# A two-layer hybrid transformer kernel: two attention blocks under way, more gate products beside the convolution, modulation over the remaining gate products

## The chip, the cores and the metric

The kernel runs on one core of a Trainium2 chip. The metric is the device time of one execution in microseconds (us), taken as the median of several runs. A core has a matrix engine (PE, with its weight loads shown as PEld), a vector engine (DVE), a scalar engine (ACT), a general engine (POOL) and a queue that issues DMA transfers (SP). Each works through its own list of instructions in order; they meet at semaphores.

## What is computed

Two layers over 512 latent tokens and 256 context tokens of width 1024, in float32. Each layer first mixes tokens with three branches that share one input projection, then runs an MLP. Layer 1, the last, computes the latent tokens alone in its mixing and MLP. Cut to the mixing sub-layer:

```python
h = layer_norm(x) * (1 + scale) + shift            # scale, shift: sections of silu(c) @ w_mod
u_pool, u_q, u_k, u_v, u_conv, u_gate = split(h @ w_in + b_in)
y_pool = pool_mixer(u_pool) @ w_pool_out
o      = attention(u_q, u_k, u_v)                  # 8 heads of 64 on 2 key/value heads
y_attn = o @ w_attn_out                            # latents: blocks of 128 queries, keys of the
                                                   # neighbouring blocks and all 256 context keys
y_conv = swish(layer_norm(depthwise_conv31(a * sigmoid(b)))) @ w_conv_out
g_pool, g_attn, g_conv = split(sigmoid(u_gate))
y = (g_pool * y_pool + g_attn * y_attn + g_conv * y_conv) @ w_out
x = layer_norm(alpha * x + gate * y) * g + b
```

The gates are 3 x 1024 columns of the input projection. The modulation has six sections (0 to 5) per layer; sections 3 and 4 are the shift and scale ahead of the MLP, and section 2 is the gate of the mixing sub-layer.

## The kernel before, in words

Every float32 matrix product is made of three products of rounded parts (high x high, high x low, low x high). A unit of weights is 128 x 512 floats: SP loads it into one of five `raw` buffers (L133), ACT rounds the high part `wh` (L138), and POOL or DVE subtracts to get the low part `wl` (L141). `wh` and `wl` live in a ring of `NRING` = 9 buffers each; in the MLP phase 4 (layer 0) or 6 (layer 1) more are added.

The order on PE is written out by hand: PE does the program's order. The other engines' orders are made by a planner at compile time. PE's program order comes from a counter of matmul columns, `pe["t"]` (L523 to L551): `tick` advances it, `later(cols, steps)` puts a piece of work into a heap that is due so many columns later, and `pace(steps, every)` issues one step of a list each time `every` columns have gone by.

In a mixing phase (`w_phase`, L559), `other` (L641) is a list of filler for PE: first the 8 gate tiles of the attention branch, then for every tile of 128 output channels the pool gate with the pool product and the convolution gate with the convolution product. One gate tile is 8 x 3 matmuls of 512 columns, and in layer 0 of 256 more. `cover(cols)` runs filler for so many columns.

The stages of a mixing phase, in PE's order:

- projections of values, keys, queries and pool;
- the depthwise convolution on DVE (L318 to L329, 31 taps). PE runs filler meanwhile: `cover(W_CONV0)` in layer 0 and `cover(W_CONV1)` in layer 1 (L739). Then come `pool_products` (L718), which for two tiles load a 128 x 128 weight (L721), split it on DVE and POOL and multiply (L730 to L732), and `conv_norm` (L331);
- attention: per key/value head four latent blocks (`attn_lat`) and, in layer 0, two context blocks (`attn_ctx`): 12 blocks in layer 0 and 8 in layer 1. A block's scores go through four heads: matmuls into one of two PSUM tiles `S` of 1024 columns, a maximum (L510) and `negm` (L511) on DVE, an exponential on ACT (L514). `softmax_pv` (L415) scales the four rows `P` (L424, L426), transposes them on PE into the same two `S` tiles (L435), splits them on ACT and DVE (L448, L449), and multiplies by the values into one bank `po` of the pool `psa` (L451, L452). One block is under way at a time: a block yields a number of columns, and `cover` fills them (L764). Ahead of the second head group the queries are projected (L761 to L763);
- `drain(other)` (L766) runs what filler is left;
- the final step (`fin`, L772 to L788): for each of 8 tiles, the attention product with the stored gate (`sgd`) and the stored sum of the other two branches (`mfd`) is added into A. In layer 0 the matmuls of modulation sections 3 and 4 (L189, 16 loads `wm` of 512 KB, 18 steps) are paced through these products, one step every 7000 columns, and the rest follows at once (L785).

PSUM has eight banks: two in `psa` (branch products, `po`, small things), two in `psg` (gate products), four as the two `S` tiles.

Of the kernel before, what the change touches and what calls it, by code (L numbers as in the profile page):

```python
# [10 lines left out]
F32 = mybir.dt.float32  # L11
F32R = mybir.dt.float32r
AF = mybir.ActivationFunctionType
ALU = mybir.AluOpType
# [24 lines left out]
NRING = 9  # L39

W_S0 = 0
W_S1 = 5200
W_S2 = 1800
W_S3 = 10000
W_PT = 4000
W_CN = 10000
W_PV = 1400
# [13 lines left out]
W_Q = 0  # L61
W_F = 2000
# [10 lines left out]
W_CONV0 = 134000  # L73
W_CONV1 = 90000
# [7 lines left out]
def backbone(ctx: ExitStack, tc: tile.TileContext, I: dict, out: bass.AP):  # L82
# [332 lines left out]
    def softmax_pv(pp, pss, g, Pt, vtiles, negm, sums, V_, sink, dst, qsl):  # L415

        es = pp.tile([P, 4], F32, tag="es", name=uid("es"), bufs=2)
        V.tensor_add(es, negm, sink[:, 4 * g:4 * g + 4])
        S.activation(es, es, AF.Exp)
        V.tensor_add(es, es, sums)  # L420
        V.reciprocal(es, es)
        for a in range(4):
            if a == 3:
                S.mul(Pt[a], Pt[a], es[:, a:a + 1])  # L424
            else:
                V.tensor_scalar(out=Pt[a], in0=Pt[a], scalar1=es[:, a:a + 1], scalar2=None, op0=ALU.mult)  # L426
        yield W_S3
        pts = []

        def transposes(ns):  # L430
            big = pss.tile([P, 1024], F32, tag="S", name=uid("pt"))
            for n in ns:
                pt = big[:, (n % 2) * 512:(n % 2 + 1) * 512]
                for a in range(4):
                    T.transpose(pt[:, a * P:(a + 1) * P], Pt[a][:, n * P:(n + 1) * P], ident)  # L435
                pts.append(pt)

        nt = len(vtiles)
        for n in range(0, min(nt, 4), 2):
            transposes(range(n, min(n + 2, nt)))  # L440
        yield W_PT
        po = bank()
        for n, vt in enumerate(vtiles):
            if n == 2 and nt > 4:
                transposes((4,))
            ph = pp.tile([P, 512], F32R, tag="pth", name=uid("pth"), bufs=2)
            pl = pp.tile([P, 512], F32R, tag="ptl", name=uid("ptl"), bufs=2)
# [12 lines left out]
        sl = (slice(None), slice(4 + 2 * g, 6 + 2 * g), qsl)  # L460
        split(dst[0][sl], dst[1][sl], ot[:, :, :], V, G)

    def attn_ctx(pp, pss, g, nb, Q, KH, KL, V_, nsink, sink, dst):

        qsl = slice(TL + nb * P, TL + (nb + 1) * P)
        s = pss.tile([P, 1024], F32, tag="S", name=uid("S"))
        for a in range(4):
            o = s[:, a * 256:(a + 1) * 256]
            T.matmul(o, Q[a][:, qsl], KH[g][:, CS], start=True, stop=False)
            T.matmul(o, Q[a][:, qsl], KL[g][:, CS], start=False, stop=True)  # L470
        negm = pp.tile([P, 4], F32, tag="ngm", name=uid("ngm"), bufs=2)
        mx = pp.tile([P, 4], F32, tag="mx", name=uid("mx"), bufs=2)
# [3 lines left out]
        sums = pp.tile([P, 4], F32, tag="sums", name=uid("sums"), bufs=2)  # L476
        Pt = []
        for a in range(4):
            p = pp.tile([P, 640], F32, tag="P", name=uid("P"), bufs=4)
            S.activation(p[:, :256], s[:, a * 256:(a + 1) * 256], AF.Exp, bias=negm[:, a:a + 1],  # L480
                         scale=SCALE, accum_out=sums[:, a:a + 1])
            Pt.append(p[:, :256])
        yield from softmax_pv(pp, pss, g, Pt, [4, 5], negm, sums, V_, sink, dst, qsl)

    def attn_lat(pp, pss, g, n, Q, KH, KL, V_, nsink, sink, dst, masks):
# [6 lines left out]
        negm = pp.tile([P, 4], F32, tag="ngm", name=uid("ngm"), bufs=2)  # L492
        mx = pp.tile([P, 4], F32, tag="mx", name=uid("mx"), bufs=2)
        sums = pp.tile([P, 4], F32, tag="sums", name=uid("sums"), bufs=2)
        Pt = []
        for a in range(4):
# [16 lines left out]
            p = pp.tile([P, 640], F32, tag="P", name=uid("P"), bufs=4)  # L513
# [3 lines left out]
            if a < 3:  # L517
                yield (W_S0, W_S1, W_S2)[a] + (W_F if a == 1 and n == 0 else 0)
# [40 lines left out]
    def w_phase(i, A, B, has_ctx, pre, todo):  # L559
# [5 lines left out]
        with ExitStack() as ph:  # L565
# [8 lines left out]
            mg = ph.enter_context(tc.tile_pool(name=f"mg{i}", bufs=4, reuse_waits="tile"))  # L574
# [27 lines left out]
            def gate_steps(m, b, w2=None, ks=()):  # L602

# [4 lines left out]
                for _, sl in outs_all:  # L608
# [3 lines left out]
                    if w2:  # L612
                        yield from branch_steps(w2, ks, ks[0], g, [(0, sl)], psa)
                return g

            def branch_steps(w, ks, w0, g, outs, pool):

                assert ks[0] in mixed
# [6 lines left out]
            def gated_steps():  # L625
# [14 lines left out]
            mixed = set()  # L640
# [111 lines left out]
            def blocks(g):  # L752
                for n in range(4):
                    yield from attn_lat(pp, pss, g, n, Q, KH, KL, V_, nsink, sink, B, masks)
                    if has_ctx and n % 2:
                        yield from attn_ctx(pp, pss, g, n // 2, Q, KH, KL, V_, nsink, sink, B)

            for g in range(NKV):
                if g:
                    Q = [kv.tile([P, W], F32R, tag=f"q{a}", name=uid("q")) for a in range(4)]  # L760
                    for jj in range(2):  # L761
                        query(Q, g, jj, pp.tile([P, TL], F32, tag="rt", name=uid("rt"), bufs=1))
                        cover(W_Q)  # L763
# [4 lines left out]
            mix.close()  # L768
            pace(None, 0)
# [408 lines left out]
```

## Time and profile before

| | us |
|---|---|
| median of 3 runs (1996.89, 1997.4, 2002.95) | 1997.4 |
| the profiled execution's own time | 1999.35 |
| its span, first to last instruction | 1997.6 |
| PE busy | 1852.4 (93%) |
| DVE busy | 1204.1 (60%) |
| POOL busy | 771.6 (39%) |
| ACT busy | 733.1 (37%) |

PE is the engine to read: a stretch in which it is idle, or runs at a granted clock below 1, is time that the span holds and no product needs. Matmuls are pipelined, so that one of 512 columns shows some 390 ns while the next starts 227 ns after it.

### The profile page before, as it was taken

The numbers are of one execution on the slowest core, as the hardware profiler recorded it, in microseconds if no ns is written. First come the engines' busy times: TensorE is split into PE (matmuls) and PEld (weight loads), VectorE is DVE, ScalarE is ACT, GpSimd is POOL, SyncE is SP. The second block draws the span as 40 slices with busy tenths as digits, with TensorE's granted clock in tenths as the row PEclk, the third lists the DMA queues.
The fourth block names the chain that finished last, engine by engine and source line by source line (L and its number), as shares of the span: only waits on it lengthen the run. The fifth ranks groups of instructions, "written<-read, shape, count | busy, mean of one in ns | idle before, by whom it ended". The sixth has DMA issues, their size and how long they took to land. (4 is left out here: it accounts for less than half of the span.)

```text
span 1997.6 us, 27087 instructions
## 1 busy us (share of the span) xinstructions
PE 1852.4 (93%) x9910; PEld 1554.4 (78%) x9910; DVE 1204.1 (60%) x2066; ACT 733.1 (37%) x1359; POOL 771.6 (39%) x630
## 2 busy tenths in 40 slices
PE   5999899998899999999999988978998989999997
PEld 4788788787678888888788868856876768888886
DVE  6489555564468946765533584886566694333356
ACT  4422245344234432232133254324545354332331
POOL 3752432332435322222222557644342554332343
PEclk9999899999999999999999989989999999999999
DMA  8523111113775434554422422231223653332331
GB/s 305 185 89 111 61 59 46 56 59 113 278 233 173 168 110 122 171 192 161 155 66 86 137 86 87 75 123 63 70 64 101 232 200 116 100 96 90 98 124 43
DMA packets 117558, 244.94 MB, mean 123 GB/s; under 512 B 14608, under 2 KB 16944, under 8 KB 117424
## 3 DMA queue, kind: packets, MB, share of 16 engines
q1 hardware_dynamic: 117424, 243.21, 37.4%
q8 instruction: 77, 1.26, 0.3%
q14 instruction: 57, 0.47, 0.1%
HBM read 223.20 MB, written 19.96 MB: 122 GB/s over the span
## 5 line engine op out<-in xcount | busy, mean ns | idle before, releaser
L141 POOL TENSOR_TENSOR wl<-raw,wh 128x512 fp32r<-128x512 f32 x372 | 517.1, 1401 | 830.9 <-ACT wh L138 803.9
L138 ACT CAST wh<-raw 128x512 fp32r<-128x512 f32 x506 | 310.4, 621 | 620.9 <-PE ps L171 282.0
L160 PE MATMUL ps<-actbh,wh 128*128 128x512 f32 (+1 forms) x1016 | 352.5, 347 | 2.8 <-ACT qf L661 1.9
L160 PE MATMUL ps<-actbl,wh 128*128 128x512 f32 (+1 forms) x1016 | 349.1, 344 | 4.0 <-POOL actbl L255 4.0
L160 PE MATMUL ps<-actbh,wl 128*128 128x512 f32 (+1 forms) x1016 | 348.1, 343 | 0.0
L160 PE MATMUL ps<-actah,wh 128*128 128x512 f32 (+1 forms) x928 | 331.7, 357 | 13.4 <-ACT actah L252 5.7
L160 PE MATMUL ps<-actal,wh 128*128 128x512 f32 (+1 forms) x928 | 327.6, 353 | 2.6 <-POOL actal L255 1.4
L160 PE MATMUL ps<-actah,wl 128*128 128x512 f32 (+1 forms) x928 | 327.1, 352 | 0.0
L160 PEld LDWEIGHTS ps<-actbh,wh 128*128 128x128 f32 x1016 | 196.1, 193 | 31.1 <-issue 4.9
L160 PEld LDWEIGHTS ps<-actbl,wh 128*128 128x128 f32 x1016 | 195.8, 193 | 25.6 <-POOL actbl L255 4.8
L160 PEld LDWEIGHTS ps<-actbh,wl 128*128 128x128 f32 x1016 | 195.2, 192 | 22.4
L160 PEld LDWEIGHTS ps<-actah,wh 128*128 128x128 f32 x928 | 177.7, 191 | 42.3 <-ACT actah L252 6.1
L160 PEld LDWEIGHTS ps<-actal,wh 128*128 128x128 f32 x928 | 177.5, 191 | 25.4 <-POOL actal L255 2.0
L160 PEld LDWEIGHTS ps<-actah,wl 128*128 128x128 f32 x928 | 177.4, 191 | 23.6
L169 PE MATMUL ps<-wh,actah 128*128 128x512 f32 x480 | 192.1, 400 | 3.4 <-DVE acc L926 2.0
L170 PE MATMUL ps<-wl,actah 128*128 128x512 f32 x480 | 189.6, 395 | 0.0
L171 PE MATMUL ps<-wh,actal 128*128 128x512 f32 x480 | 189.0, 394 | 0.5 <-DVE actal L255 0.5
L141 DVE TENSOR_TENSOR wl<-raw,wh 128x512 fp32r<-128x512 f32 x134 | 126.8, 947 | 88.8 <-ACT wh L138 88.4
L208 DVE SCALAR_TENSOR_TENSOR wm<-wm,sc,wm 128x512 f32<-128x512 f32 x140 | 120.9, 895 | 65.7 <-DMA wm<-in_wmod 65.7
L919 DVE TENSOR_TENSOR acc<-ps,acc 128x512 f32<-128x512 f32 x140 | 94.9, 684 | 93.6 <-PE ps L171 93.6
L169 PE MATMUL ps<-wh,actbh 128*128 128x512 f32 (+1 forms) x328 | 127.1, 387 | 2.2 <-DVE fg L622 2.2
L171 PE MATMUL ps<-wh,actbl 128*128 128x512 f32 (+1 forms) x328 | 126.8, 386 | 0.0
(207 smaller groups left out, 2735.2 us busy)
## 6 DMA issues: line engine op xcount, KB each, us to landing
raw<-in_w SPq DMA_DIRECT2D x264, 256.0 KB, 3.2
raw<-in_win SPq DMA_DIRECT2D x154, 256.0 KB, 2.9
wm<-in_wmod SPq DMA_DIRECT2D x72, 512.0 KB, 4.2
raw<-in_wout SPq DMA_DIRECT2D x56, 256.0 KB, 3.0
wm<-in_wmod SPq DMA_DIRECT2D x48, 256.0 KB, 5.2
raw<-in_wbr SPq DMA_DIRECT2D x32, 256.0 KB, 2.7
x1d<-R SPq DMA_DIRECT2D x10, 512.0 KB, 2.6
acc<-in_b SPq DMA_DIRECT2D x10, 512.0 KB
```

The lines of the kernel that those rows point to most:

```text
L138: S.copy(wh, r)
L141: e.tensor_tensor(out=wl, in0=r, in1=wh[:].bitcast(F32), op=ALU.subtract)
L160: T.matmul(ps, w(hl, w0 + n), x[xi][:, k, sl], start=(start and first and hl == 0 and xi == 0), stop=(stop and last and hl == 1))
L169: T.matmul(ps, x[0][:, k0 + k, tsl], wh, start=(k == 0), stop=False)
L170: T.matmul(ps, x[0][:, k0 + k, tsl], wl, start=False, stop=False)
L171: T.matmul(ps, x[1][:, k0 + k, tsl], wh, start=False, stop=(k == n - 1))
L208: V.scalar_tensor_tensor(out=o, in0=x, scalar=sc[:, k, r:r + 1], in1=o, op0=ALU.mult, op1=ALU.add)
L919: V.tensor_add(a, ps, a)
```

## The change

- The two layers' cover beside the convolution becomes 145000 (from 134000) and 118000 (from 90000) columns.
- Attention no longer runs one block after the other under `cover`. `launch` starts a block as soon as fewer than two are under way and no other is in its scores; a block's steps go into the heap (`later`) with their waits; only one block at a time is in its products (transposes and value products), another that comes to them is held. PE takes filler step by step while anything is due. The transposes and value products go in pairs of key tiles. `P` has 8 buffers instead of 4, `negm`, `mx` and `sums` 3 instead of 2.
- A gate tile is now done as a whole, and its branch product follows over both streams; before, each stream's branch product came right behind that stream's gate product.
- In layer 1 the pool gates run two tiles ahead, and the buffers of the gates grow from 4 to 6.
- The weight ring has 7 buffers instead of 9.
- The filler left after attention is no longer drained before `fin` is opened: sections 3 and 4 are paced (every 9000 columns) over that filler and the final products.

```diff
-NRING = 9
+NRING = 7
-W_S0 = 0
-W_S1 = 5200
-W_S2 = 1800
-W_S3 = 10000
-W_PT = 4000
+W_S = 3500
+W_S3 = 12000
+W_PT = 5000
-W_PV = 1400
+W_PV = 1800
-W_CONV0 = 134000
-W_CONV1 = 90000
+W_CONV0 = 145000
+W_CONV1 = 118000
...
         nt = len(vtiles)
-        for n in range(0, min(nt, 4), 2):
-            transposes(range(n, min(n + 2, nt)))
-        yield W_PT
+        yield "products", 0
         po = bank()
-        for n, vt in enumerate(vtiles):
-            if n == 2 and nt > 4:
-                transposes((4,))
...
-            S.copy(ph, pts[n])
-            V.tensor_tensor(out=pl, in0=pts[n], in1=ph[:].bitcast(F32), op=ALU.subtract)
-            w = V_[:, vt, g, :]
-            T.matmul(po, w, ph, start=(n == 0), stop=False)
-            T.matmul(po, w, pl, start=False, stop=(n == len(vtiles) - 1))
-            yield W_PV
+        for n0 in range(0, nt, 2):
+            ns = range(n0, min(n0 + 2, nt))
+            transposes(ns)
+            parts = []
+            for n in ns:
...
+                S.copy(ph, pts[n])
+                V.tensor_tensor(out=pl, in0=pts[n], in1=ph[:].bitcast(F32), op=ALU.subtract)
+                parts.append((ph, pl))
+            yield 512 * len(ns), W_PT
+            for n, (ph, pl) in zip(ns, parts):
+                w = V_[:, vtiles[n], g, :]
+                T.matmul(po, w, ph, start=(n == 0), stop=False)
+                T.matmul(po, w, pl, start=False, stop=(n == nt - 1))
+            yield 1024 * len(ns), W_PV
...
-            if a < 3:
-                yield (W_S0, W_S1, W_S2)[a] + (W_F if a == 1 and n == 0 else 0)
+            yield 2 * nk + 2 * P, W_S
+        yield None
...
-            mg = ph.enter_context(tc.tile_pool(name=f"mg{i}", bufs=4, reuse_waits="tile"))
+            mg = ph.enter_context(tc.tile_pool(name=f"mg{i}", bufs=4 if todo else 6, reuse_waits="tile"))
...
-                w, d = {}, {}
+                w, d, e, ahead = {}, {}, {}, 0 if todo else 2
+                for m in range(ahead):
+                    d[m] = yield from gate_steps(m, 0)
                 for m in range(KD + 1):
+                    if m + ahead < KD:
+                        d[m + ahead] = yield from gate_steps(m + ahead, 0)
                     if m < KD:
                         w[m] = weight_a(I["wbr"][i, m][:, 0:4 * P])
-                        d[m] = yield from gate_steps(m, 0, w[m], (0, 1))
+                        yield from branch_steps(w[m], (0, 1), 0, d[m], outs_all, side["bank"])
                     if m:
-                        e = yield from gate_steps(m - 1, 2, w.pop(m - 1), (2, 3))
+                        e = yield from gate_steps(m - 1, 2)
+                        yield from branch_steps(w.pop(m - 1), (2, 3), 2, e, outs_all, side["bank"])
...
-                for wait in blocks(g):
-                    cover(wait)
-            drain(other)
+            queue, flight = items(), {"n": 0, "scores": False, "busy": False, "products": None, "held": []}
+
+            def launch():
+                while flight["n"] < 2 and not flight["scores"] and not flight["busy"]:
...
+                    flight["n"] += 1
+                    flight["scores"] = True
+                    later(0, block_steps(x))
+
+            def block_steps(x):
+                r = next(x, 0)
+                if r is None:
+                    flight["scores"] = False
+                    later(0, block_steps(x))
+                    launch()
+                elif r == 0:
+                    flight["n"] -= 1
+                    flight["products"] = None
+                    if flight["held"]:
+                        later(0, flight["held"].pop(0))
+                    launch()
+                elif r[0] == "products":
+                    if flight["products"]:
+                        flight["held"].append(resume(x))
+                    else:
+                        yield from resume(x)
+                else:
+                    yield r[0]
+                    later(r[1], block_steps(x))
...
+            launch()
+            while pe["due"]:
+                c = next(other, None)
+                if c is None:
+                    drain(heapq.heappop(pe["due"])[2])
+                else:
+                    tick(c)
             mixed.add(4)
             mix.close()
...
+            side["bank"] = psg
             if todo:
                 pace((x for s in (3, 4) for x in mod_steps(i, s, 0, D, lambda: fin.tile(
-                    [P, D], F32, tag="wm", name=uid("wm"), bufs=4))), 7000)
+                    [P, D], F32, tag="wm", name=uid("wm"), bufs=4))), 9000)
+            drain(other)
```

## Rows read from the trace of the kernel before

**Rows 1.** Busy time by stretch: layer 0 attention, final step; layer 1 convolution, attention.

```profile
core 0: us, PE busy (x) PEld busy (x) DVE busy (x) ACT busy (x) POOL busy (x), PEclk, DMA share, GB/s
242.00:489.00 247.00, 235.96 (x1415) 206.66 (x1413) 141.69 (x278) 117.21 (x251) 73.43 (x59) 0.99 0.17 54
489.00:560.00 71.00, 54.68 (x343) 38.80 (x344) 24.70 (x37) 13.61 (x20) 27.08 (x16) 0.83 0.82 287
1310.00:1345.00 35.00, 21.87 (x86) 17.59 (x85) 27.36 (x44) 7.49 (x13) 12.07 (x13) 0.76 0.28 93
1358.00:1551.00 193.00, 175.83 (x867) 143.79 (x866) 116.14 (x212) 92.49 (x182) 67.09 (x55) 0.96 0.23 74
```

**Rows 2.** PE's waits, layer 0 attention (242 to 489): total us, times, longest.

```profile
PE pt L435 <- DVE P L426: 4.8, 4, 1.5
PE ps L160 <- ACT qf L661: 2.6, 3, 1.0
PE S L500 <- ACT P L514: 2.6, 2, 1.9
```

**Rows 3.** PE's waits, layer 1 attention (1358 to 1551).

```profile
PE pt L435 <- DVE P L426: 7.1, 6, 3.0
PE S L500 <- ACT P L514: 3.5, 2, 2.3
PE S L500 <- DVE q L673: 3.2, 2, 2.9
```

**Rows 4.** Timeline of PE, DVE and SP, end of layer 1's convolution.

```profile
1318.63 0.40 PE L730 MATMUL ps<-actah,pwh 128*128 128x512 f32 x1
...
1335.35 0.79 PE L730 MATMUL ps<-actah,pwh 128*128 128x512 f32 x1 [13.13 <-DVE pwh L254]
...
1334.01 1.28 DVE L254 CAST pwh<-pw 128x128 fp32r<-128x128 f32 x1
...
1320.41 0.38 SPq L721 DMA_DIRECT2D pw<-in_poolw  x1
```

**Rows 5.** Timeline of PE and SP, pool products of layer 0.

```profile
199.31 0.50 PE L730 MATMUL ps<-actbh,pwh 128*128 128x512 f32 x1 [1.36 <-DVE pwh L254]
...
207.85 0.50 PE L730 MATMUL ps<-actbh,pwh 128*128 128x512 f32 x1 [2.89 <-DVE pwh L254]
...
209.99 0.79 PE L732 MATMUL ps<-actbh,pwl 128*128 128x512 f32 x1 [1.22 <-POOL pwl L255]
...
203.89 0.42 SPq L721 DMA_DIRECT2D pw<-in_poolw  x1
```

**Rows 6.** Timeline of PE: gate products of layer 0, eight starts apart.

```profile
188.76 0.39 PE L160 MATMUL ps<-actah,wh 128*128 128x512 f32 x1
...
190.58 0.39 PE L160 MATMUL ps<-actah,wl 128*128 128x512 f32 x1
```

**Rows 7.** Timeline of PE and SP, final step of layer 0.

```profile
496.73 1.08 PE L189 MATMUL ps<-wm,sc 128*32 128x256 f32 x8 [8.18 <-DMA wm<-in_wmod]
...
546.35 1.08 PE L189 MATMUL ps<-wm,sc 128*32 128x256 f32 x8 [5.90 <-DMA wm<-in_wmod]
...
491.57 0.86 SPq L187 DMA_DIRECT2D wm<-in_wmod  x2
...
533.75 8.63 SPq L133 DMA_DIRECT2D raw<-in_wout  x6
```

**Rows 8.** Timeline of PE and DVE: a branch product of layer 0 and its evacuation.

```profile
220.08 0.39 PE L160 MATMUL ps<-actbh,wl 128*128 128x512 f32 x1
...
220.56 0.69 DVE L622 SCALAR_TENSOR_TENSOR sg<-sg,ps 128x512 f32<-128x512 f32 x1
```

**Rows 9.** Groups by line and shape, layer 0 attention: busy us, mean ns, idle before.

```profile
L510 DVE TENSOR_REDUCE mx<-S 128x1 f32<-128x640 f32 x16 | 13.1, 820 | 4.9 <-PE S L508 4.8
...
L514 ACT ACTIVATE P<-S,ngm 128x640 f32<-128x640 f32 x16 | 12.7, 796 | 13.3 <-DVE ngm L511 13.2
```

**Rows 10.** Costliest groups of the page, whole span: the rounding of weights.

```profile
L138 ACT CAST wh<-raw 128x512 fp32r<-128x512 f32 x506 | 310.4, 621 | 620.9 <-PE ps L171 282.0
```

More of the change, by code (lines that the diff above doesn't have):

```diff
@@ L60 @@
 E_B = 30
-W_Q = 0
-W_F = 2000
 W_PP = 2800
@@ L426, in softmax_pv @@
                 V.tensor_scalar(out=Pt[a], in0=Pt[a], scalar1=es[:, a:a + 1], scalar2=None, op0=ALU.mult)
-        yield W_S3
+        yield 0, W_S3
         pts = []
@@ L470, in attn_ctx @@
             T.matmul(o, Q[a][:, qsl], KL[g][:, CS], start=False, stop=True)
-        negm = pp.tile([P, 4], F32, tag="ngm", name=uid("ngm"), bufs=2)
-        mx = pp.tile([P, 4], F32, tag="mx", name=uid("mx"), bufs=2)
+        negm = pp.tile([P, 4], F32, tag="ngm", name=uid("ngm"), bufs=3)
+        mx = pp.tile([P, 4], F32, tag="mx", name=uid("mx"), bufs=3)
         V.tensor_reduce(out=mx, in_=s.rearrange("p (a k) -> p a k", a=4), axis=AX.X, op=ALU.max)
@@ L475, in attn_ctx @@
                                op0=ALU.mult, op1=ALU.min)
-        sums = pp.tile([P, 4], F32, tag="sums", name=uid("sums"), bufs=2)
+        sums = pp.tile([P, 4], F32, tag="sums", name=uid("sums"), bufs=3)
         Pt = []
         for a in range(4):
-            p = pp.tile([P, 640], F32, tag="P", name=uid("P"), bufs=4)
+            p = pp.tile([P, 640], F32, tag="P", name=uid("P"), bufs=8)
             S.activation(p[:, :256], s[:, a * 256:(a + 1) * 256], AF.Exp, bias=negm[:, a:a + 1],
@@ L491, in attn_lat @@
         nk = nloc * P + TC
-        negm = pp.tile([P, 4], F32, tag="ngm", name=uid("ngm"), bufs=2)
-        mx = pp.tile([P, 4], F32, tag="mx", name=uid("mx"), bufs=2)
-        sums = pp.tile([P, 4], F32, tag="sums", name=uid("sums"), bufs=2)
+        negm = pp.tile([P, 4], F32, tag="ngm", name=uid("ngm"), bufs=3)
+        mx = pp.tile([P, 4], F32, tag="mx", name=uid("mx"), bufs=3)
+        sums = pp.tile([P, 4], F32, tag="sums", name=uid("sums"), bufs=3)
         Pt = []
@@ L512, in attn_lat @@
                                    in1=nsink[:, 4 * g + a:4 * g + a + 1], op0=ALU.mult, op1=ALU.min)
-            p = pp.tile([P, 640], F32, tag="P", name=uid("P"), bufs=4)
+            p = pp.tile([P, 640], F32, tag="P", name=uid("P"), bufs=8)
             S.activation(p[:, :nk], o, AF.Exp, bias=negm[:, a:a + 1], scale=SCALE,
@@ L600, in proj, with gate_steps @@
                 return [x[0] for x in o]
-            def gate_steps(m, b, w2=None, ks=()):
+            def gate_steps(m, b):
                 t = KD * b + m
@@ L611, in gate_steps @@
                     S.activation(g[:, sl], ps, AF.Tanh, bias=bg[:, t:t + 1], scale=0.5)
-                    if w2:
-                        yield from branch_steps(w2, ks, ks[0], g, [(0, sl)], psa)
                 return g
             def branch_steps(w, ks, w0, g, outs, pool):
-                assert ks[0] in mixed
+                while ks[0] not in mixed:
+                    yield None
                 for _, sl in outs:
@@ L750, in w_phase @@
             pp = mix.enter_context(tc.tile_pool(name=f"pp{i}", bufs=1, side="right", reuse_waits="tile"))
[L752 to L763, printed above, removed]
-                for wait in blocks(g):
-                    cover(wait)
@@ L766, in w_phase, with items @@
-            drain(other)
+            def items():
+                for g in range(NKV):
+                    if g:
+                        Q[:] = [kv.tile([P, W], F32R, tag=f"q{a}", name=uid("q")) for a in range(4)]
+                        for jj in range(2):
+                            query(Q, g, jj, pp.tile([P, TL], F32, tag="rt", name=uid("rt"), bufs=1))
+                    for n in range(4):
+                        yield attn_lat(pp, pss, g, n, Q, KH, KL, V_, nsink, sink, B, masks)
+                        if has_ctx and n % 2:
+                            yield attn_ctx(pp, pss, g, n // 2, Q, KH, KL, V_, nsink, sink, B)
@@ new lines, in w_phase @@
+            queue, flight = items(), {"n": 0, "scores": False, "busy": False, "products": None, "held": []}
+            def launch():
+                while flight["n"] < 2 and not flight["scores"] and not flight["busy"]:
+                    flight["busy"] = True
+                    x = next(queue, None)
+                    flight["busy"] = False
+                    if x is None:
+                        return
+                    flight["n"] += 1
+                    flight["scores"] = True
+                    later(0, block_steps(x))
@@ L767, in w_phase, with resume @@
+            def resume(x):
+                flight["products"] = x
+                yield from block_steps(x)
+            launch()
[5 more added lines that the diff above has]
+                    tick(c)
             mixed.add(4)
             mix.close()
+            if todo:
+                for _ in pe["pace"]:
+                    pass
             pace(None, 0)
```

9 lines of the change are left out of this document (5 added, 4 removed).

## The prediction

> **What bounds the kernel now.** I read the page first: PE is busy for 93% of the span, DVE, the next, for 60%. So the time is PE's work plus the time in which PE is idle or slowed. The change leaves all of PE's products in place and only moves them; what it can be worth is read from PE's idle time and granted clock, stretch by stretch. I read busy time by stretch, then what PE waited for in each, then the timelines around the longest waits.
>
> In the four stretches of [rows 1] PE is idle for 247.0 − 236.0 = 11.0 us (layer 0 attention), 16.3 (its final step), 13.1 (the end of layer 1's convolution) and 17.2 (layer 1 attention). The column PEclk says how long the clock was at 1.2 instead of 2.4 GHz: 2 x (1 − 0.83) x 71 = 24.1 us in the final step, 16.8 at the convolution, 15.4 and 4.9 in the two attentions; work done in that time takes twice as long. These are the sums that can be won.
>
> PE runs a column in 0.444 ns: eight starts in 1.82 us, 512 columns each [rows 6].
>
> **Layer 1's convolution.** PE runs out of cover and waits 13.13 us for the second pool weight, which DVE splits only when its convolution is over, at 1334.01 [rows 4]. Cover goes in steps of 1536 columns: 90624 become 118272, and 27648 x 0.444 = 12.3 us of gate products come forward. These products would be done later in any case, so the wait they fill is a gain. PE would then reach the second pool product at 1335.35 − 13.13 + 12.3 = 1334.5. It will still wait a little. The load of that weight was issued 1.8 us after the first pool product (1320.41 against 1318.63), which itself comes 12.3 us later now; in layer 0 issue to product took 207.85 − 203.89 = 4.0 us [rows 5]. That makes 1330.9 + 1.8 + 4.0 = 1336.7, a wait of 2.2, and I leave 2.5 for the low half as well. Gain 10.6 us. Of the 16.8 us at half clock 13.1 were idle; the other 3.7 us of work lost 1.8, of which I count 1.4. Together **−12** (−14 if only the split counts; −8 if the load's delays add up as in layer 0).
>
> **Layer 0's convolution.** The cover rises from 135168 to 145152 columns, 4.4 us. That hides the first wait, 1.36 us. The two that follow, 2.89 and 1.22, hang on the second weight's load, issued at 203.89 after the first product [rows 5]; it moves along with PE, so I leave them. **−1.4** (0 to −5.5).
>
> **Layer 0's attention.** Three waits make up most of its idle time: 4.8 us for the scaled rows `P`, 2.6 for query projections, 2.6 for a score tile still being read [rows 2].
> - `P`: a block now leaves 3500 + 12000 columns (6.9 us) between its last head and the transposes, before 10000 (4.4). But the next block's heads are launched in just that time and stand in the same DVE and ACT queues. I take 4.8 down to 1.5.
> - Query projections: nothing is changed, 2.6 stays.
> - Score tiles: heads follow each other after 3500 + some 1500 columns, 2.2 us, so that a tile is wanted again after 4.4. It is held for its matmuls (1536 columns, 0.7), the maximum (0.82) and the exponential (0.80) [rows 9], 2.3 us and the hand-overs. That fits. But both blocks share the two tiles, and where the older one's transposes come between the newer one's heads, a tile is wanted again after some 2.2 to 2.8 us, with nothing to spare. Following the heap through the code, this happens about twice per latent block. I charge 0.3 us each: 16 x 0.3 = 4.8 in place of 2.6. Bounds: 0, and the longest such wait, 1.9, on each.
> - A new wait: the branch product now runs both streams back to back, each into a bank of `psa`. While `po` holds one of the two banks, the second stream must wait until DVE has emptied the first's. From the end of such a product (220.08 + 0.39) to the end of its evacuation (220.56 + 0.69) are 0.78 us [rows 8], more when DVE is taken. Following the heap, `po` is live at 7 of the 14 branch products that fall into this attention; 7 x 1.0 = 7 us. Bounds: 0, if PE finds block work in between, and 14 x 1.0.
> - Clock: of 4.9 us at half I count 1 back.
>
> Sum −3.3 + 2.2 + 7 − 1 = **+5** (−8 to +12). More density does not make another engine the bound: DVE's 141.7 us [rows 1] would lie in some 210 us in place of 247.
>
> **Layer 0's final step.** PE first waits 8.18 us for the first modulation load. It was issued at 491.57, when attention's buffers came free and SP had got that far, and took 5.2 us to its use [rows 7]. In the new order one filler step of 0.7 us comes first and the same load stands behind the same buffers. I take 5 us for what is left: −3 (0 to −6).
>
> How much filler is left there? Layer 0's filler is 24 x 8 x 3 x 768 for gates and 8 x 4 x 3 x 768 for branches, 516096 columns. Cover beside the convolution takes 145152, the pool products 19200, the normalisation 41472; attention, by the heap's rules, 285696. Only 24576 are left, 10.9 us. With the final products' 73728 columns the pace of 9000 (in effect 9216) gives 11 of 18 steps; 7000 (in effect 7680) gave 10. So the row of steps at the end shrinks only from eight to seven. Its 5.90 us wait came from SP, which stood 8.63 us on loads for the output projection ahead of the modulation loads [rows 7]; nothing in the change keeps that from happening. I count −1.5 there, and 2 of the half clock (24.1 us, at most 16.3 of them idle, so some 3.9 lost). **−6.5** (+4 if the smaller ring holds SP longer, −14 if both waits go).
>
> **Layer 1's attention.** There is one stream, so no second branch slice. 7.1 us of waits for `P` go to 3; the last block will again run without filler, since the 344064 − 158208 = 185856 columns left are used up some 7000 columns before the end. Score tiles: 16 x 0.3 = 4.8 for 3.5. The wait for the rotated queries, 3.2, stays: the second pair of heads comes 2 x 5000 columns after the projection, as before [rows 3]. Of 15.4 us at half clock I count 2 back. −4.1 + 1.3 − 2 = **−5** (−14 to +6).
>
> **The ring, 9 to 7.** ACT waited 282 us for PE to free a weight buffer [rows 10]: the ring stands full, PE does not wait for it. In the MLP phases 11 and 13 buffers remain, and a pass holds eight, so three are ahead at the start of an output projection pass instead of five. **+1** (0 to +6). Buffers of `P`, `negm` and gates cost nothing where the space is there.
>
> **Sum.** −12 − 1.4 + 5 − 6.5 − 5 + 1 = −18.9. The profiled execution took 1999.35, 2 us over the median of the runs; 1980.5 on its scale is 1978.5 on the median's. I forecast **1978 us**. About 0.3%, 6 us, is what a measurement of this kernel tells from no change.
>
> **Rivals.**
> - *Attention closes up.* The longer waits and the second block hide all but the queries and the dry end, and branch evacuations fall under block work. Idle time goes from 11.0 to 4 and from 17.2 to 7, and 5 us of clock come back: −8 and −14 in place of +5 and −5, **1956 us**. For it: DVE and ACT are under 60% busy there in layer 0 [rows 1]. Against: the new bank wait, and the same two score tiles.
> - *The modulation does not spread.* 24576 columns hold three of 18 steps. If SP's order keeps both modulation waits (0 in place of −6.5) and the convolution's second load costs its upper bound (−8), the time is **1988 us**. For it: both waits end on loads, and these follow SP's order.
> - *Two blocks starve on two score tiles.* This one ends slower. There are 60 uses of a tile in layer 0 (four heads and two or three transposes per latent block, two per context block) and 52 in layer 1. My sum has 9.6 us for them. If a use waits 0.4 us on average, that is 45 us and **2013 us**. It decides from (2003.4 − 1978)/112 = 0.23 us per use beyond my 9.6. For it: waits of up to 2.3 us occur now with one block [rows 3]. Against: they occurred four times in both layers.
>
> The Trainium skill, Perfetto Trace Analysis, section Optimization Strategy, says that the same gap repeating on the engine that should be saturated can mean that there is no room in SBUF or PSUM for the next tile. By it a second block on unchanged PSUM would repeat a gap at every use, the third rival's 2013. The trace of before, with four such waits over 64 heads (8 blocks of 4 in each layer), neither shows that state nor excludes it for two blocks.
>
> **Numbers.** Chances: the forecast 0.45 (its own range 1966 to 1990), attention closes up 0.20, the modulation does not spread 0.20 (1982 to 1996), starved blocks 0.15 (a third of it within 6 us of before). The range 1953 to 2000 leaves out some 0.1 at each end. Faster by over 0.3%: 0.45 + 0.20 + 0.13 = 0.78. Within: 0.07 + 0.05 = 0.12. Slower: 0.10.
>
> **What would show it.** Right: PE's wait for the pool weight in layer 1 falls from 13.1 to 2 to 3 us; a first wait for the modulation load of 4 to 6 us stays; new waits of about 1 us for the evacuation L622 ahead of a 256-column branch product in layer 0; attention lasts some 210 us in layer 0 and 160 in layer 1. Wrong: waits for L514 or L449 ahead of most heads or transposes; waits for weights (L141) in the MLP phases; a modulation row without waits, which would mean that SP's order changed.

## The result and the profile after

The changed kernel takes 1975.2 us, median of four runs (1971.28 to 1980.6), beside 1997.3 for the kernel before on the same chip: a ratio of 0.989, 95% interval 0.9861 to 0.9918, some 22 us faster. The forecast was 1978 us, 1953 to 2000. The profiled execution took 1975.67, its span is 1973.9 (1997.6 before); 23.7 us are to be found.

Busy time by stretch of the kernel after, for the four stretches of [rows 1]: attention and final step of layer 0, end of the convolution and attention of layer 1.

```profile
core 0: us, PE busy (x) PEld busy (x) DVE busy (x) ACT busy (x) POOL busy (x), PEclk, DMA share, GB/s
244.00:475.00 231.00, 218.97 (x1317) 190.57 (x1316) 133.22 (x269) 111.99 (x245) 68.26 (x54) 0.99 0.15 50
475.00:545.00 70.00, 60.35 (x398) 44.22 (x398) 29.52 (x43) 17.23 (x27) 30.07 (x19) 0.96 0.85 296
1318.00:1342.00 24.00, 21.28 (x89) 16.67 (x88) 15.47 (x29) 6.42 (x11) 11.56 (x11) 0.93 0.27 88
1353.00:1527.00 174.00, 158.47 (x807) 129.48 (x805) 108.21 (x208) 86.85 (x175) 63.31 (x51) 0.98 0.24 76
```

PE's idle time is the length less its busy time: 12.0, 9.7, 2.7 and 15.5 us, where it was 11.0, 16.3, 13.1 and 17.2. So idle time fell at the final step and at the convolution, and hardly in the two attentions, which the change rewrites most. PEclk rose from 0.83 to 0.96 in the final step and from 0.76 to 0.93 at the convolution: the clock came back where the waits went.

Lengths alone would mislead, since gate products moved from one stretch into another. I measure each from one landmark on PE to the next (first pool product, first score, last value product, first output product), count the columns of the gate and branch products that the two traces show between the landmarks, and take out the moved ones at 0.444 ns [rows 6]. Lengths and columns are in us:

| term | length before, after | moved in or out | change | forecast |
|---|---|---|---|---|
| layer 0, start to first score | 242.9, 244.6 | +5.1 | −3.5 | −1.4 |
| layer 0 attention | 244.5, 229.6 | −17.4 | +2.4 | +5 |
| layer 0 final step | 66.2, 69.1 | +12.3 | −9.4 | −6.5 |
| MLP of layer 0 to layer 1's first pool product | 764.9, 781.4 | +12.3 | +4.2 | +1 (the ring) |
| layer 1, pool products to first score | 40.1, 28.4 | +0.7 | −12.5 | −12 |
| layer 1 attention | 189.6, 171.9 | −13.0 | −4.8 | −5 |
| the rest | 449.2, 449.0 | 0 | −0.2 | 0 |

Moved out of layer 0's attention are 39168 columns: 11520 run ahead of it, 27648 behind its last value product. The prediction's 24576 are counted from the end of the last block, 3072 columns later. The sum of the changes is −23.7 (forecast −18.9).

The +4.2 lies in the MLP. From layer 0's first output product to the first transposition of layer 1's values PE's program is the same in all kernels of this document. The kernel before took 700.9 us there and the changed kernel 705.2; the runs built on the changed kernel took 701.4 to 709.7, each in its one profile. So a difference of a few us between two whole times can come from this stretch alone, and where it matters below, the stretches that an edit touches are given beside the whole time.

What PE waited for in the kernel after, in the same two attentions (total us, times, longest), first layer 0, then layer 1:

```profile
PE ps L156 <- DVE sg L621: 4.0, 6, 1.4
PE S L501 <- ACT P L515: 3.4, 1, 3.4
PE ps L156 <- ACT qf L665: 2.6, 3, 1.0
...
PE S L501 <- DVE q L677: 5.5, 1, 5.5
...
PE ps L452 <- DVE ptl L446: 2.7, 7, 0.8
PE ps L451 <- ACT pth L445: 2.1, 3, 0.7
PE ps L156 <- DVE sg L621: 2.0, 1, 2.0
PE S L501 <- ACT P L515: 1.4, 1, 1.4
```

The waits for the scaled rows `P`, 4.8 and 7.1 us in [rows 2, 3], are gone without a remainder. In their place stand the new wait for the evacuated branch product (`sg`, L621; the evacuation is DVE's reading of the bank, which frees it), a longer wait for the rotated queries (5.5 for 3.2), and the last block's waits (`pth`, `ptl`), which run without filler. The wait for `sg` also shows once in layer 1 (2.0 us), where the prediction had none. The score tiles cost 3.4 and 1.4.

Timeline of PE, SP and DVE in the kernel after, second pool product of layer 1, beside [rows 4]:

```profile
1324.67 0.40 PE L734 MATMUL ps<-actah,pwh 128*128 128x512 f32 x1
...
1328.24 0.50 PE L734 MATMUL ps<-actah,pwh 128*128 128x512 f32 x1
...
1331.09 0.50 PE L736 MATMUL ps<-actah,pwl 128*128 128x512 f32 x1 [2.11 <-POOL pwl L251]
...
1325.04 0.42 SPq L725 DMA_DIRECT2D pw<-in_poolw  x1
...
1327.97 0.22 DVE L250 CAST pwh<-pw 128x128 fp32r<-128x128 f32 x1
```

The weight was issued 0.4 us after the first pool product, split 2.9 us later and used at once; only its low half is late. The wait of 13.13 has become one of 2.11.

Timeline of PE and SP in the kernel after, layer 0: last value product, first modulation step, the row at the end; beside [rows 7].

```profile
474.12 0.40 PE L452 MATMUL ps<-ptl,V 128*128 128x512 f32 x1
...
478.63 0.64 PE L185 MATMUL ps<-wm,sc 128*32 128x256 f32 x8 [1.75 <-DMA wm<-in_wmod]
...
537.45 0.64 PE L185 MATMUL ps<-wm,sc 128*32 128x256 f32 x8 [3.09 <-DMA wm<-in_wmod]
...
474.52 1.38 SPq L183 DMA_DIRECT2D wm<-in_wmod  x3
...
525.89 6.45 SPq L129 DMA_DIRECT2D raw<-in_wout  x5
```

The first load is issued 0.4 us after the last value product; before, it was 4.1 us after (491.57; the last value product began at 487.46). The wait at the end has the same cause as before, SP standing on loads for the output projection, 6.45 us for 8.63.

### The profile page after: what moved, and what is told of

It is laid out like the page before. It is cut to its first block, busy times and chain, and to the rows that moved or that the text cites. A ratio compares the mean times of both kernels' runs of the same rounds, so it can differ in the third digit from the quotient of the medians.

```text
span 1973.9 us, 27007 instructions
## 1 busy us (share of the span) xinstructions
PE 1848.6 (94%) x9910; PEld 1548.4 (78%) x9910; DVE 1200.3 (61%) x2067; ACT 730.8 (37%) x1359; POOL 771.6 (39%) x629
## 5 line engine op out<-in xcount | busy, mean ns | idle before, releaser
L166 PE MATMUL ps<-wl,actbh 128*128 128x512 f32 (+1 forms) x328 | 126.8, 387 | 1.0 <-POOL wl L137 1.0
```

The costliest lines, as they stand in the source:

```text
L166: T.matmul(ps, x[0][:, k0 + k, tsl], wl, start=False, stop=False)
```

## The experiments

Differences against the changed kernel are differences of the ratios to the kernel before, times 1998 us. The interval of a single ratio is some 3 us to either side, that of the changed kernel's own 6.

### One block under way

```diff
-                while flight["n"] < 2 and not flight["scores"] and not flight["busy"]:
+                while flight["n"] < 1 and not flight["scores"] and not flight["busy"]:
```

> The changed kernel with one attention block under way instead of two; all else as changed. The theory (a second block mostly saves filler: the waits it hides would otherwise be hidden by gate products, which then lack elsewhere): layer 0 has no filler left for the final step, whose idle time goes from 9.7 back to some 15 us and whose half-clock time rises; layer 1 runs out of filler about 35 us before the end of its attention instead of 3, and two or three blocks run bare at 4 to 6 us of waits each, +12. Together +16 to +20 us over the changed kernel, 1993. Rival (the second block itself costs about as much in new waits as it saves): layer 0's attention loses its 4.0 us of waits for evacuated branch products, the dry blocks cost some 5, within 4 us of the changed kernel. Second rival (attention closes up because of the overlap itself): the waits for scaled rows come back in both layers while filler is still there, 5.3 in layer 0 and 7.4 in layer 1, +13 on top of the +16, 2005.

Measured: 2085.3 us, ratio 1.0427 (1.0408 to 1.0446), +107 us against the changed kernel. All three were far too low. Busy time by stretch, layer 0's attention and then layer 1's, each with and without filler:

```profile
245.00:400.00 155.00, 152.05 (x909) 133.57 (x908) 72.49 (x139) 67.30 (x140) 53.24 (x42) 1.00 0.19 64
400.00:455.00 55.00, 50.24 (x308) 43.91 (x306) 30.98 (x52) 21.50 (x43) 16.97 (x12) 1.00 0.18 56
455.00:540.00 85.00, 54.71 (x167) 36.55 (x167) 38.67 (x83) 27.89 (x65) 5.30 (x6) 0.60 0.06 21
1411.00:1520.00 109.00, 106.86 (x534) 89.55 (x532) 47.70 (x94) 52.00 (x101) 51.88 (x43) 1.00 0.28 90
1520.00:1635.00 115.00, 79.50 (x267) 54.44 (x267) 54.78 (x113) 36.60 (x73) 10.03 (x9) 0.66 0.10 30
```

What PE waited for in this run, layer 0, 245 to 455 us (first row, the longest of it) and 455 to 540 (the other two):

```profile
PE ps L156 <- DVE sg L621: 3.5, 4, 1.4
...
PE pt L432 <- DVE P L423: 20.1, 5, 5.2
PE ps L451 <- ACT pth L445: 7.0, 10, 0.7
```

This is the reading that matters most. Up to 455 us one block with the new, longer waits has no wait for `P` at all. The waits in columns hide the block's chain of steps, with one block or two. But a block of five key tiles now asks for 4 x 3500 + 12000 + 3 x 6800 = 46400 columns of other work (before: 5200 + 1800 + 10000 + 4000 + 5 x 1400 = 28000), and one block under way needs them all as filler. At 455 us it is used up: no gate or branch product runs from there to the end of attention, and these 85 us show wait after wait at a granted clock of 0.60; in layer 1 it is the last 115 us. With two blocks under way the same filler columns run down the waits of both, and each block's own products run down the other's. That is what the second block saves. It is not what two blocks gain over the kernel before: that one asks for fewer columns per block. The granted clock is 0.60 and 0.66 where PE is idle 30.3 of 85 and 35.5 of 115 us, and 1.00 in the stretches ahead. The Trainium skill, TensorE: Matmul & The Clock Gate, section HAM oscillation, says that waits between bursts of products let the clock fall so that the products behind each wait run at half rate; the trace agrees as far as the means of these stretches show it.

### Layer 1's cover, with two blocks and with one

```diff
 (on the changed kernel)
-W_CONV1 = 118000
+W_CONV1 = 90000
```

> The changed kernel with layer 1's cover beside the convolution back at 90000 columns. The theory: PE waits 12 to 13 us for the second pool weight again instead of 2.1, and the 27648 columns go back to attention, which then no longer runs out of filler (about 5 us of its end are saved): net +7, 1982. Rival (the cover is worth its full 12.3 us, the end of attention needs no filler): +12. Second rival (the convolution's end is set by something that comes later anyway, DVE above all): under +3.

Measured: 1990.3 us, ratio 0.9961 (0.9945 to 0.9977), +14 (8 to 21 with both intervals), nearer the rival's number. By stretch it lies between the two: from the pool products to the first score 12.1 us are lost, and attention gives back 2.7 (moved columns taken out as above), together 9.4. Another 4.0 lie in the MLP stretch of the same program (709.2 us for 705.2). The wait is the old one again, to a hundredth:

```profile
1332.12 0.79 PE L734 MATMUL ps<-actah,pwh 128*128 128x512 f32 x1 [13.12 <-DVE pwh L250]
```

The same edit alone on the kernel before:

```diff
 (on the kernel before; with the two gate products ahead and six gate buffers in layer 1)
-W_CONV1 = 90000
+W_CONV1 = 118000
```

> The kernel before with one part of the change alone: layer 1's cover of 118000 columns, with the two gate products ahead and the six buffers that it needs; one attention block under way and nine weight buffers. The theory (without a second block attention needs the filler itself): the 13.1 us wait at the convolution falls to some 2, and attention runs out of filler some 35 us before its end, which gives back 7 to 10: net -2 to -4 us, 1994. Rival (the two parts are independent): -11 to -13, 1985.

Measured: 1993.95 us, ratio 0.9978 (0.9965 to 0.9991), −4.4 us; the theory's number. Busy time by stretch of this run, convolution's end and attention in layer 1:

```profile
1320.00:1344.00 24.00, 20.33 (x93) 15.93 (x92) 15.98 (x30) 6.70 (x13) 11.62 (x11) 1.00 0.27 88
1355.00:1540.00 185.00, 165.90 (x811) 135.94 (x809) 111.39 (x209) 88.96 (x175) 61.52 (x50) 0.92 0.22 72
```

The wait at the convolution is gone here too (3.7 us idle for 13.1), but attention has 19.1 us of idle time where it had 17.2, and its clock fell from 0.96 to 0.92. From the pool products to the first score this run is 11.6 us shorter, and attention is 5.0 longer (moved columns taken out). So one edit is worth 14 us with two blocks and 4 with one in whole times, and 9.4 and 6.6 in the stretches that it touches: without these 27648 columns attention loses 2.7 us with two blocks and 5.0 with one. No run separates the second block from the other new steps of attention (pairs of key tiles, waits, buffers) in this.

### Layer 0's final step

```diff
 (drain ahead of the final step; pace 7000)
+            drain(other)
             mixed.add(4)
             mix.close()
...
-                    [P, D], F32, tag="wm", name=uid("wm"), bufs=4))), 9000)
-            drain(other)
+                    [P, D], F32, tag="wm", name=uid("wm"), bufs=4))), 7000)
```

> The changed kernel with layer 0's remaining gate products run before the final step's modulation starts, and that modulation at a pace of 7000 columns, as before the change. The theory (the final step gained because some 11 us of gate products stand behind the first modulation load and hold some of the steps): the first wait for a modulation load returns, 1.75 to some 8 us, the row of bare steps at the end is eight again, and PE runs more of it at half clock: +7 to +10, 1984. Rival (the step gained because attention now ends with SP's queue ahead, so that the loads are issued earlier): the wait stays near 2 us and the time rises by under 3.

Measured: 1976.1 us, ratio 0.989 (0.9871 to 0.9909), no difference. But here the gate products still stand between attention and the modulation, only not paced, so the next run takes all but 4608 columns of them away from there:

```diff
+            cover(24576 if has_ctx else 0)
             launch()
             while pe["due"]:
```

> The changed kernel with 24576 columns of layer 0's gate products done ahead of attention instead of behind it, so that next to nothing is left when the final step begins. The theory (the final step gained because 10.9 us of gate products stand between the last value product and the modulation, whose first load takes 5 to 8 us there): with nothing left the first wait returns from 1.75 to some 8 us and one or two more steps run bare at the end, partly at half clock: +7 to +10 over the changed kernel. Rival (the loads are merely issued earlier, since SP is ahead there now): under +2, with the first wait below 3.

Measured: 1981.0 us, ratio 0.9909 (0.9895 to 0.9922), +4, which is within the two intervals. Timeline of PE and SP, last value product, first modulation step and its load:

```profile
485.11 0.44 PE L452 MATMUL ps<-ptl,V 128*128 128x512 f32 x1
...
489.29 0.64 PE L185 MATMUL ps<-wm,sc 128*32 128x256 f32 x8 [1.19 <-DMA wm<-in_wmod]
...
484.81 0.42 SPq L183 DMA_DIRECT2D wm<-in_wmod  x1
```

The first wait is 1.19 us with next to no filler there, and PE waits 6.4 us for modulation loads in the whole step (7.4 in the changed kernel, 16.2 before). The theory fell: the gate products left over do not carry the gain. The loads come early, as the rival says. From the first pool product to the first output product this run is even 1.4 us shorter; what it lost shows in layer 0's MLP (709.7 us for 705.2, with one wait of 4.4 us for ACT ahead of a transposition, which the changed kernel lacks), and the reason for that stays open.

Why do they come early? In the kernel before SP issued the last store of the summed branches at 490.42, just as GpSimd's addition ended, and the modulation loads only behind it, at 491.57. So that store goes to another queue:

```diff
 (on the kernel before)
-                        nc.sync.dma_start(out=mfd[m - 1], in_=d.pop(m - 1))
+                        (nc.scalar if m == KD and todo else nc.sync).dma_start(out=mfd[m - 1], in_=d.pop(m - 1))
```

> The kernel before with the last store of the summed branches in layer 0 issued by ACT instead of SP, nothing else. The theory (the final step's first wait of 8.18 us came from SP, which stood behind that store until GpSimd's addition was done at 490.39, and issued the modulation loads only at 491.57): the loads are issued some 2 us earlier, behind two weight loads that end at 488.54, and the first wait falls to 5 to 6; the row of bare steps at the end keeps its wait of 5.9: -2 to -4 us. Rival (the loads wait for buffers of attention, not for SP's order): no change in issue time, -0.5 to +0.5.

Measured: 1997.7 us, ratio 1.000 (0.9988 to 1.0013). Timeline of PE and SP:

```profile
499.47 1.08 PE L189 MATMUL ps<-wm,sc 128*32 128x256 f32 x8 [7.93 <-DMA wm<-in_wmod]
...
489.06 2.47 SPq L133 DMA_DIRECT2D raw<-in_wout  x2
...
492.89 0.81 SPq L187 DMA_DIRECT2D wm<-in_wmod  x2
```

The last value product began at 490.5, so the load is issued 2.4 us after it instead of 4.1; but it now takes 6.6 us to its use instead of 5.2, and the wait stays at 7.9. The store alone is not it. Ahead of the loads SP still stands 2.47 us on two loads for the output projection, where the changed kernel has one weight load of 0.33.

The run with one block settles one more point. Timeline of PE and SP there:

```profile
540.01 0.79 PE L452 MATMUL ps<-ptl,V 128*128 128x512 f32 x1
...
540.84 0.33 SPq L183 DMA_DIRECT2D wm<-in_wmod  x1
```

With one block, too, the first load is issued at once, 0.8 us after the last value product. So the second block is not needed for it.

### What attention still waits for

The next run puts each stream's branch product right behind its own gate product in layer 0, as before the change:

```diff
-            def gate_steps(m, b):
+            def gate_steps(m, b, w2=None, ks=()):
...
                     S.activation(g[:, sl], ps, AF.Tanh, bias=bg[:, t:t + 1], scale=0.5)
+                    if w2:
+                        yield from branch_steps(w2, ks, ks[0], g, [(0, sl)], side["bank"])
...
```

> The changed kernel with each stream's branch product right behind its own gate product in layer 0, as before the change. The theory (the second stream's branch product waits for the first one's evacuation only because both run back to back while the value product holds a bank): the 4.0 us of waits for L621 in layer 0's attention and the 2.5 at its pool products go, -5 to -6 us. Rival (the evacuation is then late for the gate of the other stream, or the waits reappear at the score tiles): -1 to +2.

Measured: 1970.7 us, ratio 0.9851 (0.9837 to 0.9866), −8. The waits for `sg` are gone from layer 0's attention, 4.0 us in six, and from the stretch of the pool products ahead of it, 2.9 us in two; what PE waits for in attention now:

```profile
PE ps L452 <- DVE ptl L446: 3.2, 8, 0.9
PE ps L156 <- ACT qf L669: 2.6, 3, 1.0
PE S L501 <- ACT P L515: 1.6, 2, 1.5
```

Another run projects the queries of the second pair of heads as soon as the first pair's last scores are done:

```diff
+            def ahead_of_launch():
+                if flight["next"] is None and not flight["busy"]:
+                    flight["busy"] = True
+                    flight["next"] = next(queue, None)
+                    flight["busy"] = False
...
-                    flight["busy"] = True
-                    x = next(queue, None)
-                    flight["busy"] = False
+                    ahead_of_launch()
+                    x, flight["next"] = flight["next"], None
...
                     flight["scores"] = False
                     later(0, block_steps(x))
+                    launch()
+                    ahead_of_launch()
                     launch()
```

> The changed kernel with the queries of the second pair of heads projected as soon as the last scores of the first pair are done, not when a block leaves. The theory (the waits for rotated queries, 5.5 us in layer 1 and 2.6 in layer 0, are what keeps attention from closing up): layer 1's wait falls below 1.5, time -4 to -6. Rival (the wait moves to the next thing, the score tiles or the dry end, since layer 1's filler ends at the same place): -1 to +1.

Measured: 1963.8 us, ratio 0.9823 (0.9806 to 0.9839), −13, more than twice the theory's number. In the profile 3.8 us of it lie in the MLP stretch of the same program (701.4 us for 705.2, the shortest of the runs on the changed kernel), which no part of the edit explains. The first row is layer 0's longest wait, the others are layer 1's:

```profile
PE ps L451 <- DVE sg L621: 5.4, 1, 5.4
...
PE S L501 <- ACT P L515: 3.6, 3, 1.4
PE S L501 <- DVE q L677: 1.7, 1, 1.7
PE ps L452 <- DVE ptl L446: 1.2, 3, 0.8
```

In layer 0 one wait replaced others (a first value product now waits 5.4 us for its bank, in which DVE has still to take up a branch product), and attention got only 1.7 us shorter. In layer 1 it got 9.7 shorter: 5.5 to 1.7 for the queries, the waits at its end, where filler is used up, from 4.8 to some 2, and the clock from 0.98 to 1.00. That the projection's own 24576 columns now cover what was bare at a block's end would explain the surplus in attention over the wait removed; no run isolates it.

Two more runs have both edits together, and both with the modulation of the final step paced every 7000 columns:

```diff
-                    [P, D], F32, tag="wm", name=uid("wm"), bufs=4))), 9000)
+                    [P, D], F32, tag="wm", name=uid("wm"), bufs=4))), 7000)
```

> The changed kernel with both: each stream's branch product right behind its gate product in layer 0, and the second pair's queries projected ahead. The two remove different waits (the one the evacuated branch products, the other the rotated queries), so that their gains of 4 to 8 and 9 to 13 us should add up: -14 to -18 against the changed kernel, about 1959. Rival (both waits stand for the same slack in layer 0's attention): no better than the queries alone, 1964.

> The version with both edits, and with the modulation of layer 0's final step paced every 7000 columns instead of 9000. The theory (steps come as fast as their loads allow; the pace only moves waits from the row at the end into the spread part): within 2 us of the version with pace 9000. Rival (a faster pace leaves fewer bare steps at half clock): -3 to -5.

Measured: 1959.05 us, ratio 0.982 (0.9804 to 0.9836), −14, and 1958.2 us, ratio 0.9809 (0.9794 to 0.9823), −16. The last has the lowest median of this study, 1.9% under the kernel before and 0.8% under the changed one. That the two gains add up is not shown by the whole times: against the queries alone the stretch up to layer 0's first output product is 5.8 us shorter (536.5 for 542.3), but the code behind it, which is the same up to layer 1's first pool product, took 4.0 us longer, and it was the run with the queries alone that was short there. With pace 7000 PE's waits for modulation loads in the final step are gone; one of 3.5 us for the finished row takes their place, and the time is the same within the measurement.

### The ring alone

```diff
 (on the kernel before)
-NRING = 9
+NRING = 7
```

> The kernel before with seven weight buffers instead of nine and nothing else. The theory (the ring stands full and PE rarely waits for it): +1 to +3, as small waits for weights in the MLP phases and in the projections, where idle time rose by 2.3 us with the change. Rival (the ring holds SP back where the modulation loads stand behind weights): the final step of layer 0 gets longer by 4 to 6 us, +6. Second rival: no difference.

Measured: 2003.4 us, ratio 1.0025 (1.0011 to 1.004), +5 (2 to 8). What PE waited for between layer 0's final step and layer 1's pool products (555 to 1318 us); the kernel before has neither row there:

```profile
PE ps L160 <- DVE rs L265: 3.4, 1, 3.4
PE ps L160 <- DVE wl L141: 2.0, 2, 1.3
```

The final step of layer 0 is not longer (65.9 us for 66.2), so the first rival falls. The price of the whole run is clear of zero and larger than the waits for weights, of which only the second row is one (`rs` belongs to a norm; 0.7 us more stand behind POOL's `wl`). Where the rest lies is open: in the profile the MLP stretch of the same program is 1.9 us longer (702.8 for 700.9). The changed kernel shows rows of the same kind in that stretch, 4.2 us for `rs` and 0.7 twice for `wl`.

## Why the prediction was right, and where it was not

- **Layer 1's convolution, −12.** Right in mechanism and size: −12.5 in the profile, 12.1 back in the same stretch by undoing it alone. PE waits 2.1 us, as forecast, though for the low half; from the load's issue to the product 3.2 us went by where I reckoned 4.0.
- **Layer 1's attention, −5.** −4.8, but put together otherwise: `P` to nothing (forecast 3), score tiles 1.4 (4.8), the queries 5.5 (3.2), and 2.0 for `sg`, 2.7 and 2.1 for `ptl` and `pth`, which had no place in the sum. That the queries' wait would stay at 3.2 "as before" failed: by the code the projection now comes only when a block leaves, and that wait was the largest left. That this term came out right is in part luck.
- **Layer 0's attention, +5.** The new wait at the branch product was there, six times and 4.0 us (forecast seven and 7.0), and the run without it shows what the change paid there. Score tiles cost 3.4 us plus 0.4 (4.8 forecast), `P` nothing (1.5). So +2.4, of which idle time shows 1.0 (12.0 for 11.0). The term was over-charged, most of all at the branch product.
- **Layer 0's final step, −6.5.** −9.4. The step that failed is "the same load stands behind the same buffers", from which I took 5 us for the first wait. It was issued 3.7 us earlier relative to the last value product, and the wait was 1.75. That the leftover gate products carry the gain, which I expected of the runs, fell: the run with them done early shows that they are not needed. What moved the issue is open: it comes at once whether or not filler is left, with one block as with two, and the store's place in SP's queue does not bring it about. No run moves the loads for the output projection that stand ahead of it on SP in the kernel before.
- **Layer 0's convolution, −1.4.** −3.5, inside its range, although 2.9 us of the new wait for `sg` fall here, which the sum did not count.
- **The ring, +1.** Mis-sized: 2 to 8 us when done alone, and +4.2 in the stretch of the MLP, which differs by more than that between the runs on the changed kernel. "PE does not wait for it" was read from a ring that stands full on average; two fewer buffers show in single places.
- **The rivals.** *Starved blocks* is refuted: the score tiles cost 3.8 and 1.4 us over 112 uses, 0.05 us each where 0.23 would have decided. The Trainium skill, Perfetto Trace Analysis, section Optimization Strategy, says that a gap that keeps repeating can mean that SBUF or PSUM has no room for the next tile; the trace shows four waits in the 112 uses, so no such gap repeats here. *Attention closes up* did not happen, though two of its waits could be taken out afterwards. *The modulation does not spread* is half true: the row at the end stayed (5.6 us of waits), the first wait went.
- **The sign of right, "some 210 us in layer 0 and 160 in layer 1".** Mis-stated: by the prediction's own terms layer 0's attention, 247 us in [rows 1], less 15.3 of moved columns and plus 5, is some 237, and layer 1's, 193 less 12.3 and 5, some 176. Measured were 231 and 174.

The total, −23.7 for −18.9, is made of four terms that are off by 2 to 3 us, three of them better and one worse, so its closeness is not the closeness of each term. The largest lack lies behind the numbers. I priced two blocks by the waits that they add and remove, and found about nothing, which is near what attention measured by itself (+2.4 and −4.8). That the second block frees the filler for the convolution stood nowhere in the sum as its own term; the forecast held since the moved columns were followed through all stretches.

## What to carry to other kernels

Where one engine's idle time is filled from a fixed stock of independent work, count the stock: a second chain under way may show no gain in its own stretch and still pay, because it needs less of the stock, and the price of running out was, here, waits and a lowered clock together. Judge such an edit with its partners (the same cover cost attention 2.7 us with two blocks and 5.0 with one). After such a change read the new waits by name: two of those left here, the projection that came late and the two products that ran back to back into one pair of banks, gave another 14 to 16 us.

## What was not expected

- A stretch with filler used up costs far more than its waits: 85 us where PE was idle for 30.3, at a granted clock of 0.60, with products of 512 columns showing 0.79 us instead of 0.40. Its excess over the same attention with two blocks, some 66 us, is about 12 us of gate products done inside it and 26 of idle time; the rest, some 27 by difference, I put down to the clock.
- Moving the query projection ahead brought 13 us, 9.7 of them in layer 1's attention, against a wait of 5.5 there and 2.6 in layer 0.
- The first `wm` load of 512 KB took from 3.7 to 6.6 us from issue to use where PE waited for it. The loads for the output projection just ahead of it do not order these times: 3.7 to 4.5 us with none or one such load (one block, the changed kernel, filler early), but 4.5, 4.6, 5.2 and 6.6 with two (ring alone, cover alone, the kernel before, the store moved).
